# Two of the five wide column groups of each feed-forward input product formed from seven block products

## The chip, the core and the metric

The kernel runs on one core of one Trainium2 chip. Its engines work side by side, each through its own queue of instructions in order: the tensor engine (PE, which also loads weights, PEld), the vector engine (DVE), the scalar engine (ACT), GpSimd (POOL), and the queue that starts DMA transfers (SP). The metric is the device time of one launch in microseconds (us), from which runs of two kernels are compared. Times below are from the span's start unless said otherwise.

## The reference, cut to what matters

Four residual layers over 256 tokens of width 1024. Each has a token mixer with one wide input projection, a memory cross-attention, one output projection, and then a dense SwiGLU feed-forward:

```
def _swiglu(x, w_in, w_out):
    gu = x @ w_in
    return (jax.nn.silu(gu[..., :D_FF]) * gu[..., D_FF:]) @ w_out
...
        x = x + jnp.concatenate([mix, mo], axis=-1) @ w_o[i]
        x = x + _swiglu(_rmsnorm(x, g_ffn[i]), w_ffn_in[i], w_ffn_out[i])
```

`D_FF` is 2816, so `w_ffn_in` of a layer is 1024 x 5632: 2816 gate columns and 2816 up columns. All weights and activations are float32.

## The kernel before, in words

**Precision by parts.** Every large product is made from parts: a weight chunk `raw` is loaded (512 KB), ACT rounds it to `whi` (line 128), DVE forms the rest `wlo = raw - whi` (line 129), and PE adds three matmuls per 128 x 512 block, `hi*hi`, `hi*lo`, `lo*hi` (lines 133 to 135). The activations are transposed and split the same way once for each layer half (`transposed`, line 242: PE transposes, DVE writes `xg`, ACT `xth`, DVE `xtl`).

**Buffers.** `raw` has 3 buffers, `whi` and `wlo` have 8 each; so at most 8 chunks can stand split ahead of PE. PSUM is two pools of 4 banks: `acc` for the large products and `tr` for transposes and attention.

**The input product of the feed-forward.** The 2816 columns are taken in groups b = 0 to 4 of 512 and one of 256 (line 738). For a wide group, `proj` (line 154) runs over the gate columns and then over the up columns. One `proj` loads 4 chunks of 2 x 128 rows, and makes two passes over them, one for each half of the tokens (t = 0, 1): 8 row blocks x 3 matmuls = 24 matmuls a pass, 96 for a group. A chunk's buffer comes free when the second pass has gone over it. After a gate pass ACT forms `sg = silu(gate)` (line 752); after an up pass DVE multiplies (line 754). `hidden` (line 757) is put off by one `flush`: PE transposes the result, ACT and DVE split it into `hh` and `hl` for the output product `out_proj`.

**What sets the order.** The code is written in program order with work put off by `later` and `flush`; a scheduler then places the instructions on each engine's queue, by its own costs and by the buffers that are free. Each engine takes its queue in order, so an instruction that waits holds up all behind it. The waits between engines are set from the data and the buffers.

Of the kernel before, what the change touches and what calls it, by code (L numbers as in the profile page):

```python
# [9 lines left out]
F32 = mybir.dt.float32  # L10
F32R = mybir.dt.float32r
BF16 = mybir.dt.bfloat16
# [5 lines left out]
P = 128  # L18
# [13 lines left out]
NEG = -1e30  # L32

# [6 lines left out]
def trunk_kernel(ctx, tc, x, mem, vecs, w_in, w_kv, w_o, w_f1, w_f2, lams, g_final, out):  # L40
# [3 lines left out]
    wraw = pool("wraw", 3)  # L44
# [5 lines left out]
    ps_acc = pool("ps_acc", 4, space=PSUM)  # L50
    ps_x = pool("ps_x", 4, space=PSUM)
# [4 lines left out]
    warm = work.tile([P, 512], BF16, name="warm", tag="mk")  # L56
    nc.vector.memset(warm, 0.0)

    def warm_up(n):
        ps = ps_x.tile([P, 512], F32, name="warm_ps", tag="tr")  # L60
        for _ in range(n):
            nc.tensor.matmul(ps, warm[:, :P], warm, start=True, stop=True)
# [21 lines left out]
    tmp = work.tile([P, 3, P], F32, name="tmp", tag="att", bufs=6)[:, 0, :]  # L84
# [14 lines left out]
    def alibi(hh0):  # L99

        dist = work.tile([P, 3, P], F32, name="dist", tag="att", bufs=6)
# [14 lines left out]
    def wchunk(srcs, nk, ncol, ahead=False):  # L116
        if ahead:
            raw = big.tile([P, nk, ncol], F32, name="raw", tag="big")
        else:
            raw = wraw.tile([P, nk, ncol], F32, name="raw", tag="raw")  # L120
        c = 0
        for s in srcs:
            n = s.shape[1]
            nc.sync.dma_start(raw[:, :, c:c + n], s.rearrange("(c p) n -> p c n", p=P))
            c += n
        hi = wsplit.tile([P, nk, ncol], F32R, name="whi", tag="whi")
        lo = wsplit.tile([P, nk, ncol], F32R, name="wlo", tag="wlo")
        nc.scalar.copy(hi, raw)  # L128
        wlast[:] = [nc.vector.tensor_tensor(lo, raw, hi.bitcast(F32), ALU.subtract)]  # L129
        return hi, lo  # L130
# [9 lines left out]
    def later(rounds, f):  # L140
        pend.append([rounds, f])
# [12 lines left out]
    def proj(cols, xT, evac, start=None):  # L154

        ncol = sum(s.shape[1] for s in cols)
        nk = 1 if start else 2 if ncol == 512 else 4
        ch = []

        def load(c):  # L160
            ch.append(wchunk([s[c:c + nk * P, :] for s in cols], nk, ncol, start is not None))

        def mms(ps, t, kc):
            hi, lo = ch[kc // nk]
            return mm3(ps[:, :ncol], xT[t][0][:, kc, :], xT[t][1][:, kc, :], hi[:, kc % nk, :],
                       lo[:, kc % nk, :], kc == 0, kc == NKD - 1)

        ps = None
        done = 0
        if start:  # L170
            ps = ps_acc.tile([P, 512], F32, name="acc", tag="acc")
            done = 3
            with tc.issue_after(head[0][1]):
                load(0)
            with tc.issue_after(head[1][0]), tc.issue_after(head[1][1]):
                for kc in range(1, done):
                    load(kc * P)
            for kc in range(done):
                last = mms(ps, 0, kc)
            start(last.ins)  # L180
        for c in range(done * P, D, nk * P):
            load(c)
        for t in range(NT):
            if ps is None:
                ps = ps_acc.tile([P, 512], F32, name="acc", tag="acc")
# [6 lines left out]
            ps, done = None, 0  # L192

    def out_proj(w, order, lhs, lag, evac, settle=None):

        acc = [[ps_acc.tile([P, 512], F32, name="acc", tag="acc") for _ in range(2)] for _ in range(NT)]
        chunks = [2 * kp + k for kp in order for k in range(2)]
        n = len(chunks)

        def mms(t, h, j, ch):  # L200
            lh, ll = lhs(chunks[j], t)
            sl = slice(h * 512, (h + 1) * 512)
            mm3(acc[t][h], lh, ll, ch[0][:, 0, sl], ch[1][:, 0, sl], j == 0, j == n - 1)

        tail = []
        for j, kc in enumerate(chunks):
            ch = wchunk([w[kc * P:(kc + 1) * P, :]], 1, D)
            if j < n - 2 * lag:
                for t in range(NT):
                    for h in range(2):  # L210
                        mms(t, h, j, ch)
                flush()
            else:
                tail.append((j, ch))
        if settle is not None:
            settle()
        for t in range(NT):
            for h in range(2):
                for j, ch in tail:
                    mms(t, h, j, ch)  # L220
                flush()
                evac(t, h, acc[t][h])
# [9 lines left out]
    def stats(src):  # L232
        junk = work.tile([P, D], BF16, name="junk", tag="junk", bufs=1)
# [8 lines left out]
    def transposed(dst, src, gcol, h):  # L242

        th, tl = dst
        ps = ps_x.tile([P, 4, P], F32, name="tr", tag="tr")
# [6 lines left out]
        nc.vector.tensor_tensor(xg, ps, g, ALU.mult)  # L252
        return (nc.scalar.copy(th[:, sl, :], xg).ins,  # L253
                nc.vector.tensor_tensor(tl[:, sl, :], xg, th[:, sl, :].bitcast(F32), ALU.subtract).ins, last_pe)

    def to_T(src, dst, eng):

        ps = ps_x.tile([P, 4, P], F32, name="tr", tag="tr")
# [16 lines left out]
    def mem_kv(i):  # L275
# [3 lines left out]
        def evac(t, ps):  # L279
            kn = work.tile([P, MEMW], F32, name="mk", tag="mk")  # L280
# [4 lines left out]
        def keys(t, kn):  # L285
            tr = ps_x.tile([P, 4, P], F32, name="tr", tag="tr")
# [7 lines left out]
    def mem_attention(qT, kv):  # L294
# [5 lines left out]
        def probs(t):  # L300
            prob = work.tile([P, 4, S], F32, name="mprob", tag="mprob", bufs=1)
# [3 lines left out]
            pss = [ps_x.tile([P, 2, S], F32, name="at", tag="tr") for _ in range(2)]  # L305
# [17 lines left out]
        def turn(t, prob):  # L323
            for j0 in (0, 2):
                tr = ps_x.tile([P, 4, P], F32, name="tr", tag="tr")
# [9 lines left out]
        def values():  # L335
            for pr in range(2):
                ps = ps_x.tile([P, 2, S], F32, name="at", tag="tr")
# [32 lines left out]
    def sb_scores(qT, kT, a, then):  # L370
        zs, us = {}, {}

        def logits(h):
            z = ps_x.tile([P, 4, P], F32, name="at", tag="tr")
            nc.tensor.matmul(z[:, 0:2, :], kT[:, h, 0:P], qT[:, h, :], start=True, stop=True)  # L375
            nc.tensor.matmul(z[:, 2, :], kT[:, h, P:], qT[:, h, P:], start=False, stop=True, skip_group_check=True)
            ab = work.tile([P, 3, P], F32, name="sb_a", tag="att", bufs=6)
# [5 lines left out]
            uh = work.tile([P, 3, P], F32R, name="sb_uh", tag="att", bufs=6)  # L383
            ul = work.tile([P, 3, P], F32R, name="sb_ul", tag="att", bufs=6)
# [4 lines left out]
        def weights(h):  # L389
# [4 lines left out]
            p = work.tile([P, 3, P], F32, name="sb_p", tag="sb_p", bufs=5)  # L394
# [17 lines left out]
    def sb_values(a, v, c0, oh, ol):  # L412
        def heads(hs):
            for h in hs:
                ps = ps_x.tile([P, 4, P], F32, name="at", tag="tr")
# [11 lines left out]
    def diff_scores(qT, kT, hh0, lam, res, then):  # L427
        diffs = []
        abias = alibi(hh0)
        for e in range(2):  # L430
# [4 lines left out]
            for c in range(2):  # L435
                s = ps_x.tile([P, 4, P], F32, name="at", tag="tr")
# [3 lines left out]
                p = work.tile([P, 3, P], F32, name="df_p", tag="att", bufs=6)  # L440
# [17 lines left out]
        def turn():  # L458
            for p1 in diffs:
                tr = ps_x.tile([P, 4, P], F32, name="tr", tag="tr")  # L460
                for b in range(3):
                    nc.tensor.transpose(tr[:, b, :], p1[:, b, :], ident)
                aT = work.tile([P, 3, P], F32, name="sb_p", tag="sb_p", bufs=5)
# [6 lines left out]
    def diff_values(aTs, v, c0, oh, ol, ghead):  # L470
        ons = []
        for e in range(2):
            aT = aTs[e]
            cs = slice(c0 + e * 256, c0 + (e + 1) * 256)
            ps = ps_x.tile([P, NT, 256], F32, name="at", tag="tr")
# [12 lines left out]
        def turn():  # L488
            for e, on in enumerate(ons):
                tr = ps_x.tile([P, 4, P], F32, name="tr", tag="tr")  # L490
# [12 lines left out]
    def conv_mix(cT, uT, oh, ol, half):  # L503
        for c in range(4):
            kc = 4 * half + c
            w = [vec[:, V_CONV + 8 * k + kc:V_CONV + 8 * k + kc + 1] for k in range(3)]
            y = work.tile([P, S], F32, name="cy", tag="mk")
# [8 lines left out]
    def final():  # L516
# [4 lines left out]
        def evac(t, h, acc):  # L521
            sl = slice(h * 512, (h + 1) * 512)
            nc.vector.tensor_tensor(xs[t][:, sl], acc, xs[t][:, sl], ALU.add)
            junk = work.tile([P, D], BF16, name="junk", tag="junk", bufs=1)
# [44 lines left out]
    def load_mem():  # L569
        for t, mt in enumerate(mem_in):  # L570
# [5 lines left out]
            junk = work.tile([P, D], BF16, name="junk", tag="junk", bufs=1)  # L576
# [26 lines left out]
    for i in range(DEPTH):  # L603
# [10 lines left out]
        def memory():  # L614
            mqT = big.tile([P, 2, 2, S], F32R, name="mqT", tag="big")

            def evac(t, ps):
                n = work.tile([P, MEMW], F32, name="mk", tag="mk")
# [3 lines left out]
            def queries(t, n):  # L622
                tr = ps_x.tile([P, 4, P], F32, name="tr", tag="tr")
# [97 lines left out]
        def residual(gcol, nxt, rnx):  # L721
            def evac(t, h, acc):
# [4 lines left out]
                later(1, lambda: transposed(nxt[t], xs[t], gcol, h))  # L727
# [4 lines left out]
        nxt, rnx = [], []  # L732
        out_proj(w_o[i], [4, 0, 1, 2, 3], o_lhs, 2, residual(V_FFN + 8 * i, nxt, rnx), drain)
# [4 lines left out]
        for b in range(6):  # L738
# [18 lines left out]
            def hidden(t, s, hh, hl, n):  # L757
                tr = ps_x.tile([P, 4, P], F32, name="tr", tag="tr")
# [9 lines left out]
            if n == 512:  # L768
                proj([gcols], xT, lambda t, ps: h_out(t, ps, None))
                proj([ucols], xT, lambda t, ps: h_out(t, None, ps))  # L770
            else:
                proj([gcols, ucols], xT, lambda t, ps: h_out(t, ps[:, :n], ps[:, n:2 * n]))

# [39 lines left out]
```

## Time and profile before

| what | value |
|---|---|
| time, median of 3 runs | 1306.28 us (1306.04 to 1307.22) |
| the profiled execution's own time | 1305.36 us |
| its span | 1303.7 us |
| granted PE clock, whole span | 0.999 |
| DVE busy in the span | 762.2 us |
| ACT busy in the span | 672.3 us |
| HBM read | 225.23 MB |

The profile is of one execution. "Busy" of an engine is the sum of its instructions' durations; matmuls overlap one another in the array, so a matmul's duration is longer than the time between two starts. A row of the timeline gives the start, the duration, the engine, the source line, the output and inputs, and in brackets how long the engine stood idle before it and whom it waited for.

### The profile page before, as it was taken

Reading aid. Unit: us, or ns where it says so; the run is one execution under the profiler, and the core shown is the slowest. Engines: PE = TensorE matmul, PEld = TensorE weight load, DVE = VectorE, ACT = ScalarE, POOL = GpSimd, SP = SyncE. Lnnn points to the kernel's source line nnn. Section 1 sums busy time; section 2 is a strip of 40 time slices with the busy share of each in tenths; the row PEclk is TensorE's granted clock in tenths of the full one; section 3 lists DMA queues with packets and bytes.
Section 4 is the critical chain, followed back from the end, with each engine's and each line's share of the span. In section 5 each row is a group of like instructions: output and inputs, shape, how many; then the busy total and the mean of one; then the engine's idle time right before and its main releaser. Section 6 shows DMA issues by size and latency. Waiting matters only on the chain.

```text
span 1303.7 us, 16267 instructions
## 1 busy us (share of the span) xinstructions
PE 1288.5 (99%) x6175; PEld 1065.3 (82%) x6175; DVE 762.2 (58%) x955; ACT 672.3 (52%) x943; POOL 52.0 (4%) x109
## 2 busy tenths in 40 slices
PE   8899999999999999999999999999999999999997
PEld 6788888888888888888888888888888888888886
DVE  5675565655576656555457776555546655655542
ACT  6656454444456545444445455444436755544441
POOL 1000000000101000000000000000000001000001
PEclk9999999999999999999999999999999999999999
DMA  6654565657564456665655565656665445656571
GB/s 243 194 155 136 162 193 178 188 177 218 152 186 123 144 162 194 194 193 179 202 154 174 174 185 172 187 176 186 209 190 171 129 129 162 187 183 184 183 220 44
DMA packets 107790, 227.34 MB, mean 174 GB/s; under 512 B 7488, under 2 KB 20288, under 8 KB 107712
## 3 DMA queue, kind: packets, MB, share of 16 engines
q1 hardware_dynamic: 107712, 226.31, 56.8%
q8 instruction: 48, 0.79, 0.2%
q14 instruction: 30, 0.25, 0.1%
HBM read 225.23 MB, written 1.05 MB: 174 GB/s over the span
## 4 chain that ended last, share of the span: by engine, by line
PE 93%; DMA 3%; DVE 2%; ACT 1%; issue 0%; POOL 0%; SPq 0%; POOLq 0%; ACTq 0%; DVEq 0%
PE acc L133 28%; PE acc L135 28%; PE acc L134 28%; DMA raw<-in_w_in 2%; PE tr L760 1%; PE tr L248 1%; PE tr L260 1%; DVE wlo L129 1%; PE at L341 1%; ACT whi L128 1%; PE tr L328 1%; PE at L309 1%; PE at L417 1%; PE at L392 0%; PE at L375 0%
## 5 line engine op out<-in xcount | busy, mean ns | idle before, releaser
L129 DVE TENSOR_TENSOR wlo<-raw,whi 128x1024 fp32r<-128x1024 f32 (+1 forms) x428 | 518.5, 1215 | 395.5 <-ACT whi L128 386.7
L128 ACT CAST whi<-raw 128x1024 fp32r<-128x1024 f32 (+1 forms) x428 | 445.0, 1044 | 415.4 <-PE acc L135 265.2
L133 PE MATMUL acc<-whi,xth 128*128 128x512 f32 (+1 forms) x1152 | 454.0, 394 | 1.2 <-ACT xth L253 1.2
L134 PE MATMUL acc<-wlo,xth 128*128 128x512 f32 (+1 forms) x1152 | 442.5, 384 | 1.8 <-DVE wlo L129 1.8
L135 PE MATMUL acc<-whi,xtl 128*128 128x512 f32 (+1 forms) x1152 | 443.4, 385 | 0.0
L135 PEld LDWEIGHTS acc<-whi,xtl 128*128 128x128 f32 x1152 | 216.4, 188 | 44.0
L134 PEld LDWEIGHTS acc<-wlo,xth 128*128 128x128 f32 x1152 | 217.0, 188 | 42.6 <-DVE wlo L129 3.0
L133 PEld LDWEIGHTS acc<-whi,xth 128*128 128x128 f32 x1152 | 216.7, 188 | 42.2 <-ACT xth L253 1.7
L133 PE MATMUL acc<-whi,hh 128*128 128x512 f32 x320 | 125.4, 392 | 0.0
L135 PE MATMUL acc<-whi,hl 128*128 128x512 f32 x320 | 124.6, 389 | 0.0
L134 PE MATMUL acc<-wlo,hh 128*128 128x512 f32 x320 | 124.6, 389 | 0.0
L135 PEld LDWEIGHTS acc<-whi,hl 128*128 128x128 f32 x320 | 60.1, 188 | 12.6
L133 PEld LDWEIGHTS acc<-whi,hh 128*128 128x128 f32 x320 | 60.1, 188 | 12.2
L134 PEld LDWEIGHTS acc<-wlo,hh 128*128 128x128 f32 x320 | 60.1, 188 | 12.1
L752 ACT ACTIVATE sg<-acc,rstd 128x512 f32<-128x512 f32 (+1 forms) x48 | 31.4, 654 | 49.5 <-PE acc L135 49.5
L133 PE MATMUL acc<-whi,oh 128*128 128x512 f32 x128 | 51.1, 399 | 0.0
L135 PE MATMUL acc<-whi,ol 128*128 128x512 f32 x128 | 50.0, 391 | 0.0
L134 PE MATMUL acc<-wlo,oh 128*128 128x512 f32 x128 | 49.9, 390 | 0.0
L754 DVE SCALAR_TENSOR_TENSOR sg<-acc,rstd,sg 128x512 f32<-128x512 f32 (+1 forms) x48 | 33.8, 703 | 26.6 <-PE acc L135 18.8
L235 ACT ACTIVATE junk<-x 128x1024 bf16<-128x1024 f32 x16 | 16.9, 1058 | 36.8 <-DVE x L724 36.5
L228 POOL TENSOR_SCALAR rstd<-ss 128x1 f32<-128x1 f32 x16 | 5.3, 334 | 640.2 <-ACT junk L235 640.1
L724 DVE TENSOR_TENSOR x<-acc,x 128x512 f32<-128x512 f32 x28 | 19.3, 688 | 18.9 <-PE acc L135 18.4
(185 smaller groups left out, 1071.0 us busy)
## 6 DMA issues: line engine op xcount, KB each, us to landing
raw<-in_w_ffn_in SPq DMA_DIRECT2D x160, 512.0 KB, 4.3
raw<-in_w_in SPq DMA_DIRECT2D x100, 512.0 KB, 4.2
raw<-in_w_ffn_out SPq DMA_DIRECT2D x88, 512.0 KB, 4.3
raw<-in_w_o SPq DMA_DIRECT2D x40, 512.0 KB, 4.4
raw<-in_w_mem_kv SPq DMA_DIRECT2D x16, 512.0 KB, 3.8
raw<-in_w_ffn_in SPq DMA_DIRECT2D x32, 256.0 KB, 3.7
raw<-in_w_in SPq DMA_DIRECT2D x8, 256.0 KB, 6.2
x<-in_x SPq DMA_DIRECT2D x4, 256.0 KB, 4.0
```

The lines of the kernel that those rows point to most:

```text
L128: nc.scalar.copy(hi, raw)
L129: wlast[:] = [nc.vector.tensor_tensor(lo, raw, hi.bitcast(F32), ALU.subtract)]
L133: nc.tensor.matmul(ps, lh, wh, start=first, stop=False)
L134: nc.tensor.matmul(ps, lh, wl, start=False, stop=False)
L135: return nc.tensor.matmul(ps, ll, wh, start=False, stop=last)
L235: nc.scalar.activation(junk, src, AF.Square, accum_out=ss)
L248: last_pe = nc.tensor.transpose(ps[:, c, :], src[:, kc * P:(kc + 1) * P], ident).ins
L260: nc.tensor.transpose(ps[:, c, :], src[:, c * P:(c + 1) * P], ident)
L309: nc.tensor.matmul(pss[r][:, pr, :], qT[r * 64:(r + 1) * 64, a, pr, t * P:(t + 1) * P], kT[r * 64:(r + 1) * 64, b, pr, :], start=a + b == ...
L724: nc.vector.tensor_tensor(xs[t][:, sl], acc, xs[t][:, sl], ALU.add)
L752: nc.scalar.activation(s, g_ps, AF.Silu, scale=rx[t])
L754: nc.vector.scalar_tensor_tensor(s, u_ps, rx[t], s, ALU.mult, ALU.mult)
```

## The change

For b = 1 and b = 4 of every layer the two `proj` calls are replaced by `winograd`, Strassen's scheme in a form with shared sums. It treats [gate columns | up columns] of the group as a 2 x 2 block matrix: the rows of the weights in two halves of 512 (`b11`, `b21` gate, `b12`, `b22` up), against the tokens in two halves and their 1024 channels in two halves. Seven products of blocks take the place of eight. A product is 4 row blocks x 3 matmuls = 12 matmuls, in two steps (s = 0, 1) of 6; a group has 84.

Three kinds of work come with it. Four sums of weight blocks are formed on DVE in each step (`plus`, 128 x 1024), before their split. `tokens_side` makes four sums of token blocks once for each layer, and splits them. `h_sums` puts the seven accumulators together into gate and up on DVE. The seven accumulators of a group live in seven PSUM banks, so the two PSUM pools become one of 8 banks. `raw` gets 7 buffers instead of 3, and most small work tiles share one set of 12 (`att`). The bytes that are loaded stay the same.

```
-    wraw = pool("wraw", 3)
+    wraw = pool("wraw", 7)
...
-    ps_acc = pool("ps_acc", 4, space=PSUM)
-    ps_x = pool("ps_x", 4, space=PSUM)
+    ps_x = ps_acc = pool("ps", 8, space=PSUM)
...
+    def winograd(left, right, ab, evac):
+        acc = {}
+        def product(p, w, s):
+            if s == 0:
+                acc[p] = ps_acc.tile([P, 512], F32, name="acc", tag="ps")
+            lh, ll = ab[p]
+            for k in range(2):
+                kc = 2 * s + k
+                mm3(acc[p], lh[:, kc, :], ll[:, kc, :], w[0][:, k, :], w[1][:, k, :], kc == 0, kc == 3)
+            if s == 1:
+                evac(p, acc)
...
+        def plus(out, a, b):
+            nc.vector.tensor_tensor(out, a, b, ALU.add)
+        for s in range(2):
+            b11, b12 = (load(c, 2 * s * P) for c in (left, right))
+            b21, b22 = (load(c, 512 + 2 * s * P) for c in (left, right))
+            product(1, wparts(b11), s)
+            t = wraw.tile([P, 2, 512], F32, name="wsum", tag="raw")
+            plus(t, b11, b12)
+            product(5, wparts(t), s)
+            flush()
+            product(2, wparts(b21), s)
+            plus(t, t, b22)
+            product(6, wparts(t), s)
+            flush()
+            plus(b12, b12, b22)
+            product(7, wparts(b12), s)
+            product(3, wparts(b22), s)
+            flush()
+            plus(t, t, b21)
+            product(4, wparts(t), s)
...
+            if b in (1, 4):
+                def h_sums(p, acc, sums=sums, sg=sg, hh=hh, hl=hl):
+                    def up(t, c):
+                        nc.vector.scalar_tensor_tensor(sg[t], c, rneg[t], sg[t], ALU.mult, ALU.mult)
+                        later(2, lambda: hidden(t, sg[t], hh, hl, 512))
+                    if p == 1:
+                        nc.scalar.copy(sums["v"], acc[1])
+                    elif p == 2:
+                        tt(sg[0], acc[2], sums["v"], ALU.add)
+                        nc.scalar.activation(sg[0], sg[0], AF.Silu, scale=rx[0])
+                    elif p == 6:
+                        tt(sums["u"], acc[6], sums["v"], ALU.add)
+                        tt(sums["x"], acc[5], sums["u"], ALU.add)
+                    elif p == 7:
+                        tt(sums["u"], acc[7], sums["u"], ALU.add)
+                        tt(sums["y"], acc[5], sums["u"], ALU.add)
+                    elif p == 3:
+                        tt(sums["x"], acc[3], sums["x"], ALU.add)
+                        up(0, sums["x"])
+                    elif p == 4:
+                        tt(sg[1], acc[4], sums["u"], ALU.add)
+                        nc.scalar.activation(sg[1], sg[1], AF.Silu, scale=rx[1])
+                        up(1, sums["y"])
+                winograd(gcols, ucols, ab, h_sums)
```

On DVE, where group b = 1 of the first layer ended and b = 2 began, this stood before. `wlo_2028` is the last up chunk of b = 1, `wlo_2097` to `wlo_2115` are the four gate chunks of b = 2, and `sg_1922` is the first multiply of b = 1.

```order
L129 TENSOR_TENSOR wlo_2028<-raw_2025,whi_2027 128x1024
L764 TENSOR_TENSOR hl_1751<-tr_1961,hh_1750 128x4x128
L129 TENSOR_TENSOR wlo_2097<-raw_2094,whi_2096 128x1024
L129 TENSOR_TENSOR wlo_2103<-raw_2100,whi_2102 128x1024
L129 TENSOR_TENSOR wlo_2109<-raw_2106,whi_2108 128x1024
L129 TENSOR_TENSOR wlo_2115<-raw_2112,whi_2114 128x1024
L754 SCALAR_TENSOR_TENSOR sg_1922<-acc_2031,rstd_1523,sg_1922 128x512
```

At the same place of the DVE queue now: `wlo_1933`, `wlo_1946` and `wlo_1959` are the splits of products 7, 3 and 4 in step 1 of b = 1, and `wlo_1978` is the first gate chunk of b = 2.

```order
L859 TENSOR_TENSOR sg_1773<-acc_1818,sv_1890 128x512
L132 TENSOR_TENSOR wlo_1933<-raw_1874,whi_1932 128x1024
L863 TENSOR_TENSOR su_1927<-acc_1830,sv_1890 128x512
L132 TENSOR_TENSOR wlo_1946<-raw_1878,whi_1945 128x1024
L864 TENSOR_TENSOR sx_1928<-acc_1800,su_1927 128x512
L132 TENSOR_TENSOR wlo_1959<-wsum_1892,whi_1958 128x1024
L867 TENSOR_TENSOR su_1927<-acc_1842,su_1927 128x512
L870 TENSOR_TENSOR sx_1928<-acc_1853,sx_1928 128x512
L868 TENSOR_TENSOR sy_1942<-acc_1800,su_1927 128x512
L852 SCALAR_TENSOR_TENSOR sg_1773<-sx_1928,rneg_1767,sg_1773 128x512
L873 TENSOR_TENSOR sg_1774<-acc_1865,su_1927 128x512
L132 TENSOR_TENSOR wlo_1978<-raw_1975,whi_1977 128x1024
```

The next group's first split stood ahead of all of the group's multiplies; now it stands behind the whole putting together of the group (`L859` to `L873`), of which the last, `L873`, waits for the last product.

At the end of b = 4, DVE goes on to the narrow group b = 5, whose four chunks are `wlo_2525`, `wlo_2532`, `wlo_2539` and `wlo_2546`.

```order
L864 TENSOR_TENSOR sx_2475<-acc_2347,su_2474 128x512
L132 TENSOR_TENSOR wlo_2532<-raw_2528,whi_2531 128x1024
L867 TENSOR_TENSOR su_2474<-acc_2389,su_2474 128x512
L870 TENSOR_TENSOR sx_2475<-acc_2400,sx_2475 128x512
L868 TENSOR_TENSOR sy_2489<-acc_2347,su_2474 128x512
L852 SCALAR_TENSOR_TENSOR sg_2320<-sx_2475,rneg_1767,sg_2320 128x512
L873 TENSOR_TENSOR sg_2321<-acc_2412,su_2474 128x512
L132 TENSOR_TENSOR wlo_2539<-raw_2535,whi_2538 128x1024
L852 SCALAR_TENSOR_TENSOR sg_2321<-sy_2489,rneg_1769,sg_2321 128x512
L132 TENSOR_TENSOR wlo_2546<-raw_2542,whi_2545 128x1024
```

Here two of the next group's four chunks stand ahead of the last sums and two behind them; before, all four stood ahead of the first multiply of b = 4.

On SP, the queue that starts the loads, this stood early in the program before: `raw_313` is the last chunk of the first key projection, `memn` the memory tokens, `raw_437` the first chunk of the values, `raw_547` that of the memory keys and values.

```order
L124 DMA raw_313<-in_w_in 128x2x512
L566 DMA memn_291<-in_mem 128x1024
L566 DMA memn_293<-in_mem 128x1024
L124 DMA raw_437<-in_w_in 128x2x512
L124 DMA raw_443<-in_w_in 128x2x512
L124 DMA raw_449<-in_w_in 128x2x512
L124 DMA raw_455<-in_w_in 128x2x512
L124 DMA raw_547<-in_w_mem_kv 128x2x512
```

The same place now, where `raw_310` is the last key chunk and `raw_434` the first of the values:

```order
L124 DMA raw_310<-in_w_in 128x2x512
L124 DMA raw_434<-in_w_in 128x2x512
L124 DMA raw_440<-in_w_in 128x2x512
L124 DMA raw_446<-in_w_in 128x2x512
L124 DMA raw_452<-in_w_in 128x2x512
L640 DMA memn_288<-in_mem 128x1024
L640 DMA memn_290<-in_mem 128x1024
L124 DMA raw_544<-in_w_mem_kv 128x2x512
```

The loads of the values moved ahead of the memory tokens.

More of the change, by code (lines that the diff above doesn't have):

```diff
@@ new lines, in tokens_side, with parts @@
+    def tokens_side(xg, xT):
+        a11, a12, a21, a22 = xg[0][0], xg[0][1], xg[1][0], xg[1][1]
+        half = lambda t, h: tuple(x[:, 4 * h:4 * h + 4, :] for x in xT[t])
+        ab = {1: half(0, 0), 2: half(0, 1), 4: half(1, 1)}
+        tt, stt = nc.vector.tensor_tensor, nc.vector.scalar_tensor_tensor
+        def parts(src):
+            hi = work.tile([P, 4, P], F32R, name="sh", tag="att", bufs=NATT)
+            lo = work.tile([P, 4, P], F32R, name="sl", tag="att", bufs=NATT)
+            nc.scalar.copy(hi, src)
+            tt(lo, src, hi.bitcast(F32), ALU.subtract)
+            return hi, lo
+        tt(a22, a22, a21, ALU.subtract)
+        ab[5] = parts(a22)
+        tt(a21, a11, a21, ALU.subtract)
+        ab[7] = parts(a21)
+        stt(a11, a22, -1.0, a11, ALU.mult, ALU.subtract)
+        ab[6] = parts(a11)
+        stt(a12, a12, -1.0, a11, ALU.mult, ALU.subtract)
+        ab[3] = parts(a12)
+        return ab
@@ L194, in out_proj @@
     def out_proj(w, order, lhs, lag, evac, settle=None):
-        acc = [[ps_acc.tile([P, 512], F32, name="acc", tag="acc") for _ in range(2)] for _ in range(NT)]
+        acc = [[ps_acc.tile([P, 512], F32, name="acc", tag="ps") for _ in range(2)] for _ in range(NT)]
         chunks = [2 * kp + k for kp in order for k in range(2)]
@@ L726, in evac @@
                     nxt.append(xt_tiles())
[L727 removed]
+                    if keep is not None:
+                        keep.append([])
+                later(1, lambda: transposed(nxt[t], xs[t], gcol, h, None if keep is None else keep[t]))
                 if h == 1:
@@ L772, in trunk_kernel @@
                 proj([gcols, ucols], xT, lambda t, ps: h_out(t, ps[:, :n], ps[:, n:2 * n]))
+            if b == 0:
+                ab = tokens_side(xg, xT)
+                rneg = []
+                for t in range(NT):
+                    r = small.tile([P, 1], F32, name="rneg", tag="rneg")
+                    nc.vector.tensor_scalar(r, rx[t], -1.0, None, ALU.mult)
+                    rneg.append(r)
         def f_lhs(kc, t):
```

93 lines of the change are left out of this document (54 added, 39 removed).

## The prediction

> **What bounds the kernel now.** I read the page's busy line and its chain first, then the timeline of PE in the feed-forward of the first layer, since that is where the change sits.
>
> ```profile
> PE 1288.5 (99%) x6175; PEld 1065.3 (82%) x6175; DVE 762.2 (58%) x955; ACT 672.3 (52%) x943; POOL 52.0 (4%) x109
> PE 93%; DMA 3%; DVE 2%; ACT 1%; issue 0%; POOL 0%; SPq 0%; POOLq 0%; ACTq 0%; DVEq 0%
> L133 PE MATMUL acc<-whi,xth 128*128 128x512 f32 x1088 | 435.6, 401 | 1.2 <-ACT xth L253 1.2
> 171.52 0.39 PE L133 MATMUL acc<-whi,xth 128*128 128x512 f32 x1
> 176.74 0.39 PE L135 MATMUL acc<-whi,xtl 128*128 128x512 f32 x1
> 185.13 0.60 PE L760 MATMUL tr<-ident,sg 128*128 128x128 f32 x4
> 185.48 0.48 PE L133 MATMUL acc<-whi,xth 128*128 128x512 f32 x1
> 188.34 0.39 PE L133 MATMUL acc<-whi,xth 128*128 128x512 f32 x1
> ```
>
> PE is the chain, and it hardly ever waits. But what a matmul costs is not its duration of 0.39 to 0.40 us. The rows at 171.52 and 176.74 are the first and the last of the 24 matmuls of one pass, so one starts every 5.22 / 23 = **0.227 us**. By the duration, 96 matmuls would be worth 38 us; by the distance of starts, 21.8. Four transposes cost 0.35 (185.13 to 185.48). Group b = 1 of the first layer starts at 188.34.
>
> Next the two engines that feed PE, and the same stage by windows (columns: length, then busy time and count of PE, PEld, DVE, ACT, POOL, the clock, the DMA share, GB/s).
>
> ```profile
> L129 DVE TENSOR_TENSOR wlo<-raw,whi 128x1024 fp32r<-128x1024 f32 x420 | 513.1, 1225 | 394.6 <-ACT whi L128 385.9 <-PE tr L625 0.6
> L128 ACT CAST whi<-raw 128x1024 fp32r<-128x1024 f32 x420 | 440.1, 1052 | 409.3 <-PE acc L135 265.2 <-DMA raw<-in_w_ffn_in 59.3 <-DMA raw<-in_w_in 23.3
> L754 DVE SCALAR_TENSOR_TENSOR sg<-acc,rstd,sg 128x512 f32<-128x512 f32 x40 | 29.9, 748 | 18.8 <-PE acc L135 18.8
> L724 DVE TENSOR_TENSOR x<-acc,x 128x512 f32<-128x512 f32 x28 | 19.3, 688 | 18.9 <-PE acc L135 18.4
> L254 DVE TENSOR_TENSOR xtl<-xg,xth 128x512 fp32r<-128x512 f32 x32 | 22.2, 697 | 6.8 <-ACT xth L253 6.6
> 188.30:211.10 22.80, 22.80 (x106) 18.84 (x105) 12.55 (x13) 10.97 (x13) 0.00 (x0) 1.00 0.61 187
> 45.54 2.36 DVE L129 TENSOR_TENSOR wlo<-raw,whi 128x1024 fp32r<-128x1024 f32 x2
> 47.81 0.56 DVE L381 SCALAR_TENSOR_TENSOR sb_a<-at,sb_a 128x384 f32<-128x384 f32 x1
> 166.14 0.69 DVE L252 TENSOR_TENSOR xg<-tr,vec 128x512 f32<-128x512 f32 x1
> 166.74 0.68 DVE L724 TENSOR_TENSOR x<-acc,x 128x512 f32<-128x512 f32 x1
> 171.71 1.22 DVE L129 TENSOR_TENSOR wlo<-raw,whi 128x1024 fp32r<-128x1024 f32 x1
> ```
>
> In a group of 22.8 us DVE works 12.55 and ACT 10.97: a chunk is split in 1.1 us and serves PE for 12 matmuls, 2.7 us. Rows of a full DVE queue follow faster than they last: two splits fill 45.54 to 47.81, **1.14 us each**, and a row of 512 fills 166.14 to 166.74, **0.60**. A three-operand row (0.748) I take at 0.66, by the same overlap.
>
> **The change: what goes.** 12 matmuls for each group, two groups, four layers: 96 x 0.227 = **21.8 us** of PE. The DMA bytes stay.
>
> **What comes, and on whom.** In a Strassen group PE needs 84 x 0.227 + 0.35 = 19.4 us. DVE needs 14 splits and 8 sums of weight blocks at 1.14 (25.1), 7 sums of accumulators at 0.60 and two multiplies at 0.66 (5.5), two `hl` (1.2): about 32 us. A split chunk now serves PE for 6 matmuls, 1.36 us, and costs DVE 1.14 plus 4/7 of a sum, 1.8. So for these 19 us **DVE is the slower engine**, and the 8 split buffers decide how far it gets ahead. ACT has 14 casts and five smaller rows, about 18 us, and just keeps pace.
>
> *First group (b = 1).* DVE comes to its first new row (`L256`) when the last split of b = 0 is through, 171.71 + 1.14 = 172.85. Up to and with the first split of b = 2, which the order puts behind `L873`, there stand 15 splits and 8 sums (26.2 us), 15 rows of 512 with `tokens_side` among them (9.0), 5 three-operand rows (3.3) and one small (0.1): 38.6. One wait inside can't be avoided: the split of product 6 in step 1 comes right behind the sum it splits, and ACT's cast (1.052 less overlap) lies between, 1.0 us. So that split ends at 172.85 + 38.6 + 1.0 = 212.5. PE without a wait would ask for it at 188.34 + 19.4 + 0.23 = 208.0. PE is 4.6 us late, with the restart. 0.35 of that is filled by transposes that stood elsewhere before, and b = 2's third chunk comes 0.1 late behind the second multiply: **4.3 us given back** against 2.7 won. After that b = 2 and b = 3 leave DVE some 10 us each, so nothing is carried on.
>
> *Second group (b = 4).* No `tokens_side`, and DVE starts from a full set of buffers. Its last wait is for the buffer of b = 3's first up chunk, free after six matmuls of the last pass; with the cast that is 3.15 us before b = 4 begins. Then 9 splits, 4 sums, two rows of 512 and a multiply stand up to the first row of `h_sums` (`L859`): 16.7 us, so DVE is there 13.55 us after the group's start. Product 2 is complete at 14.25 (10 products, a transpose, 0.26 until the result is seen), so DVE waits 0.7 us. From there the rows up to the third chunk of b = 5 (`wlo_2539`) are 4 splits, 7 sums, 1 multiply, 9.4 us after product 2's result, which is 0.26 after its last matmul's successor starts. PE comes there after 4 products, 2 chunks, a transpose and one matmul, 8.75. Late by 1.05 with the restart; the fourth chunk is late by 0.7, its multiply waiting on ACT's silu. **1.8 us given back.**
>
> The four layers' orders on DVE and ACT are alike row by row in this stage, so both count four times: 17.2 and 7.2 us.
>
> *The front.* More `raw` buffers and the loads of the values moved ahead touch the waits between 40 and 60 us.
>
> ```profile
> 41.96 0.38 PE L375 MATMUL at<-qT,kT 128*128 128x256 f32 x1
> 43.95 0.49 PE L376 MATMUL at<-qT,kT 128*128 128x128 f32 x2 [1.40 <-DVE kT L264]
> 56.92 0.39 PE L135 MATMUL acc<-whi,meml 128*128 128x512 f32 x1
> 59.57 0.44 PE L392 MATMUL at<-sb_uh,ntri 128*128 128x384 f32 x1 [2.26 <-ACT sb_uh L385]
> 49.64 1.05 ACT L128 CAST whi<-raw 128x1024 fp32r<-128x1024 f32 x1 [1.98 <-DMA raw<-in_w_in]
> 52.48 1.05 ACT L128 CAST whi<-raw 128x1024 fp32r<-128x1024 f32 x1 [1.38 <-DMA raw<-in_w_in]
> 55.00:60.00 5.00, 2.74 (x12) 1.82 (x11) 3.28 (x4) 3.56 (x7) 1.69 (x2) 1.00 0.66 197
> ```
>
> PE loses 1.99 - 0.23 and 2.65 - 0.23, 4.2 us in all. ACT's queue waited 1.98 + 1.38 us for loads ahead of the `sb_uh` that the second gap waits for; with 7 buffers those loads start earlier, and that gap should go. In the first, one split (1.14) no longer stands ahead of the `kT` copy. **3.4 us won**, between 0 and 4.2.
>
> *Not shown by any row:* the sum of two weight blocks, all SBUF, float32 out. Its nearest row is the split, the same operation and size (1.14); lower end 0.60, as if at twice the rate; upper end 1.35, a three-operand row of that size and a wait on the row before. I take 1.14. At 0.60 the 8 sums of b = 1 shrink by 4.3 us and the stall is gone (-17 us in four layers); at 1.35 b = 1 ends 1.7 us later (+7). In b = 4 no sum of weights stands between `L859` and the late splits, so either end moves only its margin of 0.7.
>
> The Trainium skill, page "VectorE: DVE Perf Modes", section "The perf-mode tier table", has a two-tensor operation on fp32 at one element a cycle even in SBUF, and only one-source operations at two. By it the sum stays as it is and the lower end falls away; by the rows alone 0.60 stays possible, since none shows this operation.
>
> PSUM in one pool costs nothing that I can find: when product 4's accumulator opens, seven others were taken, and the transposes' bank was emptied 3 us before.
>
> **Sum.** 1305.36 (the profiled execution) - 21.8 + 17.2 + 7.2 - 3.4 = 1304.6. The median of the runs is 0.9 above that execution: **1305.5 us**, no change that can be told. About 0.2% (2.6 us) is what a measurement of this kernel tells from none.
>
> **Rivals.**
>
> *DVE keeps up.* If the lag at the group ends is a half of what I worked out (sums nearer to 0.9 us, or fewer exposed casts), 12 us come back: 1293. For it: DVE is only 58% busy over the span. Against it: 32 us of rows in 19.4 us of PE, and 8 buffers. Fully hidden it would be 1281, and by the matmuls' durations, 38 us instead of 21.8, even 1265; the sum of DVE's rows speaks against the one, the distance of starts against the other.
>
> *The casts are exposed more often (slower).* Eight products of a group split a sum that DVE has just made, so ACT's cast (1.05) lies between two DVE rows each time; I counted one exposed hop in b = 1 and none in b = 4. The point from which it decides is b = 4's margin of 0.7 us and ACT's load of 18 in 19.4: once ACT is behind, every hop shows. Three more in each group cost 3 x 1.05 x 8 = 25, less 3 for margins: 1328. For it: L129 waited 385.9 us for `whi` in the span, its main wait. Against it: other rows stand between most pairs.
>
> *The clock falls in the gaps (slower).* The row of 55 to 60 us shows PE idle for 2.65 us and the clock at 1.00. The longest single gap I expect is about 1.5 us, so nothing. Were it half for some 3.4 us behind each of the 8 group ends, it would cost 8 x 1.7 = 14 us, 1319. The Trainium skill, page "TensorE: Matmul & The Clock Gate", section "Why this matters for your kernels", warns of the half rate after idle gaps over about 3 us; no gap here is that long before the change.
>
> *The front gains nothing:* 1308.9. It is inside the forecast's own range, 1300 to 1311.
>
> **Chances.** Forecast 0.45; DVE keeps up, at least by half, 0.25; casts exposed 0.25; clock 0.05. For eight in ten the range reaches into both neighbours, 1288 to 1324. Faster by over 0.2% (under 1303.7): all of the second case and about a quarter of the forecast's, 0.37. Within: 0.27. Slower: both last cases and the forecast's top, 0.36.
>
> **What would show it.** Right: PE gaps of 4 to 5 us in sum just behind each b = 1 and of about 2 behind each b = 4, waiting on `wlo`; DVE near 100% from 173 to 213; a pitch of 1.14 for the sums; no gap at 57. Wrong: gaps inside the groups rather than behind them (casts), or hardly any (DVE ahead); a clock under 1.00.

## The result, and the profile after

The changed kernel takes **1335.03 us** (median of 4, 1333.75 to 1336.26) against 1306.16 of the kernel before in the same comparison: ratio 1.0222, 95% interval 1.0204 to 1.0239. It is slower by 29 us; the forecast was 1305.5, and the range ended at 1324. The profiled execution has a span of 1334.5 us, 30.8 more than before.

The page of the changed kernel: the busy line, the clock by slices, and the chain.

```profile
PE 1290.3 (97%) x6079; PEld 1056.6 (79%) x6079; DVE 930.3 (70%) x1163; ACT 721.1 (54%) x1015; POOL 60.0 (4%) x109
PEclk9989999999999999999998999999999899999999
PE 76%; DVE 16%; issue 3%; ACT 2%; DMA 1%; SPq 0%; POOL 0%; POOLq 0%; ACTq 0%; DVEq 0%
```

PE has fewer matmuls, yet the chain is only 76% PE, and the clock row has an 8 in three slices. The waits of PE in the whole span (total, times, longest) say on whom it waited:

```profile
PE acc L136 <- ACT whi L131: 17.6, 4, 4.4
PE acc L137 <- DVE wlo L132: 13.4, 21, 1.1
PE tr L836 <- DVE sg L852: 4.1, 4, 1.0
```

The second and third rows are, for the most part, the group ends that the prediction spoke of. The first is four waits of 4.4 us that it did not. One lies in each layer's mixer; PE's timeline in the first:

```profile
85.18 1.03 PE L402 MATMUL tr<-ident,mprob 128*128 128x128 f32 x8
86.14 0.97 PE L383 MATMUL at<-mkT,mqT 64*128 64x256 f32 x12
91.52 0.80 PE L136 MATMUL acc<-whi,xth 128*128 128x512 f32 x1 [4.41 <-ACT whi L131]
92.11 0.63 PE L334 MATMUL tr<-ident,qkn 128*128 128x128 f32 x2
93.11 0.80 PE L137 MATMUL acc<-wlo,xth 128*128 128x512 f32 x1 [0.36 <-DVE wlo L132]
```

Behind the wait a matmul lasts 0.63 to 0.80 us instead of 0.39. The windows (length, then busy time and count of each engine, clock, DMA share, GB/s) have for 90 to 105 us in the changed kernel

```profile
90.00:105.00 15.00, 13.12 (x52) 10.04 (x54) 11.27 (x16) 10.11 (x15) 0.00 (x0) 0.77 0.61 194
```

and in the kernel before

```profile
90.00:105.00 15.00, 15.00 (x93) 11.77 (x92) 11.40 (x22) 8.26 (x20) 0.00 (x0) 1.00 0.50 148
```

So a stall costs its 4.8 us of waiting and then some 3 us more at half clock. The stages are told apart by starts of the same PE work in both timelines:

| stage | rows compared | after minus before, layers 1 to 4 (us) | sum |
|---|---|---|---|
| front | first scores of the memory attention, 78.18 for 82.65 | -4.5 | -4.5 |
| mixers | from there (L309, now L383) to the values (L341, now L415); first layer 82.65 to 101.31, now 78.18 to 104.60 | +7.8, +7.6, +8.0, +8.0 | **+31.4** |
| b = 1 | first `sg` transposes of b = 0 to those of b = 2; first layer 185.13 to 230.58, now 188.75 to 237.28 | +3.1, +1.5, +1.6, +2.9 | +9.2 |
| b = 4 | from the first `sg` transposes of b = 2 to the last `sg` transposes of b = 5; first layer to 293.57, now 299.46 | -0.8, -1.5, -1.7, -0.8 | -4.8 |

Together 31.3, of 30.8 in the span. The mixers are the loss: the other three stages cancel one another.

**Why the mixers.** The diff holds a line that the account of the change leaves out and that the prediction gave no term: `mprob`, the probabilities of the memory attention, left its own buffer and takes its turn among `raw`'s seven.

```
-            prob = work.tile([P, 4, S], F32, name="mprob", tag="mprob", bufs=1)
+            prob = wraw.tile([P, 4, S], F32, name="mprob", tag="raw")
```

ACT's queue in the first mixer shows what follows. Before, the casts stand between the exponentials (`L316`) of the two token halves; `whi_955` to `whi_973`, of the chunks used first, stand further ahead:

```
L128 CAST whi_1073<-raw_1071 128x1024
L316 ACTIVATE mprob_844,msm_846<-at_847,mmx_845 128x256 x2
L316 ACTIVATE mprob_844,msm_846<-at_848,mmx_845 128x256 x2
L128 CAST whi_1079<-raw_1077 128x1024
L128 CAST whi_1085<-raw_1083 128x1024
...
L316 ACTIVATE mprob_921,msm_923<-at_924,mmx_922 128x256 x2
```

Now six casts, from that of the very next projection (`whi_952`) on, stand behind both, and so it is in all four mixers:

```
L390 ACTIVATE mprob_918,msm_920<-at_921,mmx_919 128x256 x2
L390 ACTIVATE mprob_918,msm_920<-at_922,mmx_919 128x256 x2
L131 CAST whi_952<-raw_950 128x1024
L131 CAST whi_958<-raw_956 128x1024
...
L131 CAST whi_1076<-raw_1074 128x1024
```

The timeline of DVE, ACT and SP beside PE's wait:

```profile
87.14 1.29 DVE L386 TENSOR_REDUCE mmx<-at 128x2 f32<-128x512 f32 x2
88.60 0.47 ACT L390 ACTIVATE mprob<-at,mmx 128x256 f32<-128x256 f32 x1 [1.98 <-DVE mmx L387]
90.41 5.78 ACT L131 CAST whi<-raw 128x1024 fp32r<-128x1024 f32 x6
51.96 10.53 SPq L124 DMA_DIRECT2D raw<-in_w_in  x3
86.24 8.34 SPq L124 DMA_DIRECT2D raw<-in_w_in  x3
```

PE computes the scores (86.14), DVE their maximum (87.14), ACT the exponentials (88.60), and only then ACT casts the chunk for PE's next matmul (90.41). Five of the six chunks' loads had been started by 62.5 us, so it isn't data that is missing: a chain of three engines that used to run beside the projection now stands ahead of it in ACT's order. The sixth load did wait, until the transposes `L402` had freed the first `mprob`. That the casts stand there because buffers of one set are handed out in program order, and `mprob` asks before the next chunks, is my reading of the order; that they stand there only while `mprob` is in the set, the experiments show.

### The profile page after: what moved, and what is told of

It reads as the page before. It is cut to its first block, busy times and chain, and to the rows that moved or that the text cites. A ratio compares the mean times of both kernels' runs of the same rounds, so it can differ in the third digit from the quotient of the medians.

```text
span 1334.5 us, 16363 instructions
## 1 busy us (share of the span) xinstructions
PE 1290.3 (97%) x6079; PEld 1056.6 (79%) x6079; DVE 930.3 (70%) x1163; ACT 721.1 (54%) x1015; POOL 60.0 (4%) x109
## 4 chain that ended last, share of the span: by engine, by line
PE 76%; DVE 16%; issue 3%; ACT 2%; DMA 1%; SPq 0%; POOL 0%; POOLq 0%; ACTq 0%; DVEq 0%
PE acc L137 23%; PE acc L138 23%; PE acc L136 23%; DVE wlo L132 7%; DVE wsum L221 2%; ACT whi L131 1%; PE tr L334 1%; DMA raw<-in_w_ffn_out 1%; PE tr L836 1%; PE tr L320 1%; DVE raw L221 1%; DVE sl L253 1%; PE at L415 1%; PE at L449 1%; PE at L491 1%
## 5 line engine op out<-in xcount | busy, mean ns | idle before, releaser
L131 ACT CAST whi<-raw 128x1024 fp32r<-128x1024 f32 (+1 forms) x428 | 436.9, 1042 | 277.0 <-PE acc L138 215.5
L136 PE MATMUL acc<-whi,xth 128*128 128x512 f32 (+1 forms) x992 | 396.5, 400 | 18.0 <-ACT whi L131 17.6
L137 PE MATMUL acc<-wlo,xth 128*128 128x512 f32 (+1 forms) x992 | 388.0, 391 | 13.4 <-DVE wlo L132 13.4
L138 PE MATMUL acc<-whi,xtl 128*128 128x512 f32 (+1 forms) x992 | 385.5, 389 | 0.0
L136 PEld LDWEIGHTS acc<-whi,xth 128*128 128x128 f32 x992 | 189.6, 191 | 56.1 <-ACT whi L131 20.1
L137 PEld LDWEIGHTS acc<-wlo,xth 128*128 128x128 f32 x992 | 189.8, 191 | 54.1 <-DVE wlo L132 20.1
L136 PE MATMUL acc<-whi,hh 128*128 128x512 f32 x320 | 125.4, 392 | 0.0
L131 ACT CAST whi<-wsum 128x1024 fp32r<-128x1024 f32 x48 | 50.5, 1052 | 55.8 <-DVE wsum L221 52.0
L136 PEld LDWEIGHTS acc<-whi,hh 128*128 128x128 f32 x320 | 60.1, 188 | 12.2
L132 DVE TENSOR_TENSOR wlo<-wsum,whi 128x1024 fp32r<-128x1024 f32 x48 | 58.5, 1218 | 5.9 <-ACT whi L131 5.5
L137 PE MATMUL acc<-wlo,sh 128*128 128x512 f32 x128 | 50.7, 396 | 0.7
L136 PE MATMUL acc<-whi,oh 128*128 128x512 f32 x128 | 51.1, 399 | 0.0
L138 PE MATMUL acc<-whi,sl 128*128 128x512 f32 x128 | 49.9, 390 | 0.0
L136 PE MATMUL acc<-whi,sh 128*128 128x512 f32 x128 | 49.2, 389 | 0.0
```

The source lines that it names most:

```text
L136: nc.tensor.matmul(ps, lh, wh, start=first, stop=False)
L137: nc.tensor.matmul(ps, lh, wl, start=False, stop=False)
L138: return nc.tensor.matmul(ps, ll, wh, start=False, stop=last)
```

## The experiments

Theory A: `mprob` among `raw`'s buffers costs the 31 us. B: the single PSUM pool and the shared small tiles do. C: Strassen itself does. Times are medians; each ratio is to the kernel before on the same chip.

**1. `mprob` in its own buffer** (6 `raw` buffers, to make room).

```
-    wraw = pool("wraw", 7)
+    wraw = pool("wraw", 6)
-            prob = wraw.tile([P, 4, S], F32, name="mprob", tag="raw")
+            prob = work.tile([P, 4, S], F32, name="mprob", tag="mprob", bufs=1)
```

> The changed kernel with one edit: mprob gets a work buffer of its own again, and raw 6 buffers instead of 7 to make room. Theory A (the ring): mprob sits among raw's buffers, so the load that is given mprob's buffer waits until the transposes L402 have read it, and every later load waits behind it on SP; the four waits of about 4.4 us on whi in the mixers, with the half clock behind them, are worth 31.4 us. Expected 1335.0 - 31.4 = 1303.6 us, give or take 2 for the buffer less; no PE wait on whi over 1 us and a clock of 1.00 from 75 to 105 us. Theory B (one PSUM pool and one set of small tiles): the mixers lose because scores, transposes and accumulators take turns in 8 banks. Expected 1335 +- 2, the waits stay. Theory C (Strassen itself): 1335, since nothing of it is changed.

Measured: 1307.76 us, ratio 1.0011 (1.0002 to 1.0020). PE's waits:

```profile
PE acc L137 <- DVE wlo L132: 12.0, 19, 1.1
PE tr L836 <- DVE sg L852: 4.1, 4, 1.0
PE acc L136 <- ACT xth L327: 1.5, 1, 1.5
```

The first mixer's window:

```profile
90.00:105.00 15.00, 15.00 (x82) 11.58 (x81) 9.35 (x18) 8.69 (x18) 0.00 (x0) 1.00 0.43 134
```

The four waits and the half clock are gone with one tile out of the set; as causes of the 31 us, B and C fall. The expectation took the held-up load for the cause. By the rows above, the chunk that PE waits for had been loaded, and it is the place of its cast on ACT that costs. The time is 4 us above what A gave: by the starts of the table, the feed-forward stages cost 6.5 us here against 4.4, and the mixers 1.4.

**2. Only that line, in the kernel before** (`raw` 4 instead of 3, `mprob` among them).

> The kernel before (no Strassen, two PSUM pools of 4, its own tags) with one edit: mprob takes its turn among raw's buffers, which are 4 instead of 3, so the bytes stay the same. Theory A: the mixers stall as in the changed kernel, four times by at least 4 us and the half clock behind: 1306.2 + 31 = 1337 us, at least 1326. Theories B and C: 1306 +- 2, since neither the PSUM pool nor Strassen is there.

Measured: 1324.33, ratio 1.0142 (1.0127 to 1.0158). Without any Strassen, PE stalls again in each mixer, here at the transposes of `mprob`:

```profile
PE tr L328 <- DVE mprob L320: 10.7, 3, 3.6
PE tr L328 <- ACT whi L128: 3.8, 1, 3.8
```

A holds in kind, but 18 us is under its 20. By the first scores of the memory attention (78.02 for 82.65), the front gains 4.6 us here too, which the expectation left out; so the rest of the kernel loses some 23. The waits are 0.6 to 0.8 us shorter, and the clock, at half for 6.8 us behind each wait in the changed kernel, is at half for as long in the first layer only (0.50 from 89.30 to 96.10) and for half as long in the other three (0.75 over 6.8 us).

**3 and 4. No Strassen**, with `mprob` in the set, and out of it.

```
-            if b in (1, 4):
+            if b in ():
```

> The changed kernel with all five wide groups by proj: no Strassen and no sums of tokens, but its buffers, tags and PSUM pool. From the lag of the one trace behind the other, b = 1 cost 9.2 us in the four layers and b = 4 gained 4.8, so theories A and B expect 1335.0 - 4.4 = 1330.6 us with the four long waits on whi in place. Theory C expects the time to fall back to 1302 to 1306.

> Both edits: mprob in a buffer of its own with 6 for raw, and no Strassen. Theory A expects the kernel before less what the front won in the changed trace (4.5 us): 1301.5 us, so Strassen as it stands would be worth about +2 us beside own6. Theory B expects 1330, the waits in the mixers staying. Theory C expects 1302 to 1306.

Measured: 1330.41, ratio 1.0189 (1.0175 to 1.0202), and 1301.81, ratio 0.9968 (0.9956 to 0.9981). Both are within 0.3 us of A; B had the first as well, but not the second. `PE acc L136 <- ACT whi L131` is 17.6 us in the first and absent in the second. So the buffers other than `mprob`'s win 4.5 us (the front), and Strassen as it stands loses 4 to 6, more than the 2 that was expected.

**5 and 6. Strassen in one group**, `b in (4,)` or `b in (1,)`, with `mprob` apart.

> mprob in its own buffer, raw 6, Strassen in b = 4 alone. Theory A with the lags of the trace: b = 4 gained 0.8 to 1.7 us a layer, 4.8 in all, so 1301.8 - 4.8 = 1297.0 us. If the gain of b = 4 were only what b = 1 had pushed on to it, it would be 1301.8 or more.

> The same with Strassen in b = 1 alone. b = 1 cost 1.5 us in two layers and 3 in the two where the clock fell behind it, 9.2 in all: 1301.8 + 9.2 = 1311.0 us; with no fall of the clock 1308; if b = 1 and b = 4 share one cost (DVE's backlog carried on), 1302.

Measured: 1298.55, ratio 0.9951 (0.9939 to 0.9964), and 1311.32, ratio 1.0048 (1.0035 to 1.0062). The times are within 1.6 us of what was worked out, but for b = 4 this flatters it: the kernel before is 1.5 us faster on this chip (1304.86 for 1306.33), and by the ratios b = 4 gains about 2 us over run 4 (0.9951 for 0.9968, whose intervals overlap). By the starts of the stages it gains 0.8 to 0.9 us in each layer, 3.2 in all, and not 4.8. With b = 1 alone, the stage of b = 4 takes 63.0 us in every layer, as before: b = 1 hands no cost on, and the two groups don't share one. b = 4 alone is faster than the kernel before and than the changed one.

**7. Strassen in b = 2 and 4**, so that `tokens_side` lies under an ordinary group.

> The same with Strassen in b = 2 and b = 4: the sums of tokens and their splits, 8 DVE rows and more, now stand under b = 1, an ordinary group that leaves DVE some 10 us. If the 4.3 us behind b = 1 came from tokens_side on top of the group's own rows, b = 2 behaves as b = 4 and the time is 1301.8 - 9.6 = 1292 us. If they come from the group's own rows and the place of the next group's splits behind the last sums, b = 2 costs as b = 1 did: 1301.8 + 9.2 - 4.8 = 1306.

Measured: 1301.12, ratio 0.9968 (0.9956 to 0.9981): between the two, and the same as run 4 without any Strassen. Of the first layer's waits:

```profile
230.94 0.50 PE L137 MATMUL acc<-wlo,xth 128*128 128x512 f32 x1 [0.88 <-DVE wlo L132]
232.86 0.66 PE L836 MATMUL tr<-ident,sg 128*128 128x128 f32 x4 [0.26 <-DVE sg L852]
273.84 0.66 PE L836 MATMUL tr<-ident,sg 128*128 128x128 f32 x4 [0.50 <-DVE sg L852]
275.58 0.50 PE L137 MATMUL acc<-wlo,xth 128*128 128x512 f32 x1 [1.08 <-DVE wlo L132]
```

Without `tokens_side` beside it a group's end waits less than b = 1's did (1.6 us in sum for 2.4), but behind b = 4 PE waits longer than with b = 4 alone (1.9 us for 1.3). That one ordinary group between does not let DVE catch up wholly is a likely reason, not tested by itself.

**8. The wait filled** with 18 matmuls that nobody reads, `mprob` in the set.

```
             prob = probs(1)
+            fps = ps_x.tile([P, 4, P], F32, name="fill", tag="ps")
+            for _ in range(18):
+                nc.tensor.matmul(fps, fillx[0][0][:, 0, :], fillx[0][0][:, 0:4, :], start=True, stop=True)
```

> The changed kernel, mprob still in raw's ring, with 18 matmuls of 512 columns that nobody reads put into PE's queue right where it waits for whi in each mixer. At 0.227 us between starts they fill 4.1 us of the wait of 4.41. If the half clock behind the wait comes from PE standing idle, it stays at 1.00 and some 3 us a mixer come back (14 matmuls at 0.43 instead of 0.227): 1335.0 - 12 = 1323 us. If the clock falls from something else there (the burst of loads), 1335 and the clock of 90 to 105 us still at 0.77. If the fill is worked off before the wait begins or after it, the time rises by 4 x 4.1 = 16.

Measured: 1327.57, ratio 1.0169 (1.0155 to 1.0182), 4.6 us above what was expected. On PE's timeline the fill in the second layer, and a wait that is new there:

```profile
386.32 4.37 PE L429 MATMUL fill<-xth 128*128 128x512 f32 x18
...
411.54 0.30 PE L539 MATMUL tr<-ident,df_p 128*128 128x128 f32 x1 [2.71 <-DVE df_p L531]
```

The first mixer's window:

```profile
90.00:105.00 15.00, 14.82 (x80) 11.21 (x79) 13.11 (x20) 11.29 (x18) 0.00 (x0) 1.00 0.70 241
```

The clock stays at 1.00, and second scores to values shrink by 3.0 us in the first mixer (86.09 to 101.58, for 86.14 to 104.60): the fall came from PE standing idle, and is worth what was said. In the second layer some 4.5 us are given back at the new wait and a half clock behind it: the run was 4.9 us ahead of the changed kernel at that layer's first scores, won 2.7 in the stall, and was 3.1 ahead at its feed-forward. Why that wait came is open.

**9 and 10. One of four sums of weights on POOL**, with b = 1 and 4, and with b = 4 alone.

```
-            plus(b12, b12, b22)
+            nc.gpsimd.tensor_tensor(b12, b12, b22, ALU.add)
```

> mprob in its own buffer, raw 6, Strassen in b = 1 and 4, and in each step one of the four sums of weight blocks (b12 + b22, for product 7) on POOL instead of DVE: 2 x 1.14 us of DVE a group less. If DVE's sum of rows sets both group ends, the 2.4 us of waits behind b = 1 and the 1.2 to 1.4 behind b = 4 nearly go: 1307.8 - 4 x 3.3 - 2 for a clock that no longer falls = 1293 us. POOL's sum is estimated at 2.6 us, twice the 1.29 us of its row of 128x512 at L602; product 7 comes some 5 us after its loads, so it should be covered. If POOL's sum takes much longer than that or slows DVE while it runs, product 7 waits, and the time is 1308 or more.

> The same with Strassen in b = 4 alone. The waits of 1.3 us behind b = 4 go, the matmuls saved (2.7 us) stay: 1298.6 - 4 x 1.2 = 1293.8 us. If the last two splits of b = 5 are late by their place behind the last sum (L873) and not by the rows ahead of it, 1298.6.

Measured: 1323.10, ratio 1.0138 (1.0120 to 1.0156), and 1308.75, ratio 1.0025 (1.0016 to 1.0034): slower by 15 and 10 us than with DVE. Run 9's groups of POOL's sums and of DVE's splits `sl`:

```profile
L235 POOL TENSOR_TENSOR raw<-raw 128x1024 f32<-128x1024 f32 x16 | 48.1, 3008 | 328.3 <-DVE wsum L221 256.7 <-DVE sg L830 53.6 <-DMA raw<-in_w_ffn_in 18.0
L253 DVE TENSOR_TENSOR sl<-xg,sh 128x512 fp32r<-128x512 f32 x16 | 19.5, 1220 | 0.0
```

The same `sl` in run 1:

```profile
L253 DVE TENSOR_TENSOR sl<-xg,sh 128x512 fp32r<-128x512 f32 x16 | 10.9, 684 | 0.0
```

And run 9's timeline where the first of these sums runs:

```profile
170.54 3.99 POOL L235 TENSOR_TENSOR raw<-raw 128x1024 f32<-128x1024 f32 x1 [3.21 <-DVE wsum L221]
...
172.24 2.85 DVE L253 TENSOR_TENSOR sl<-xg,sh 128x512 fp32r<-128x512 f32 x1
```

POOL's sum takes 3.0 us in the mean, and a DVE row beside it 2.85 instead of 0.68. What DVE is spared it loses again: it has 16 rows fewer and is busy for 936.0 us, for 931.8 in run 1. How the 15 us come about from there was not followed; by the starts, some 10 of them are lost in the stage of b = 4.

**11 and 12. The next group's first chunks split ahead of the last evacuation**: two of them with b = 1 and 4, and three with b = 4 alone.

```
             plus(t, t, b21)
-            product(4, wparts(t), s)
+            parts = wparts(t)
+            if s == 1:
+                ahead = [wchunk(*n) for n in nxt]
+            product(4, parts, s)
```

> mprob in its own buffer, raw 6, Strassen in b = 1 and 4 with all sums on DVE, and the first two chunks of the next group loaded and split ahead of product 4's evacuation, so that on DVE behind b = 1 both splits stand ahead of L873 instead of behind it. If the place behind L873 makes the split late, some 1 us a layer comes back behind b = 1: 1303.8 us. If DVE's sum of rows sets it, one row of 0.6 us and the wait on the last product change places: within 1306 to 1308.5.

> mprob in its own buffer, raw 6, Strassen in b = 4 alone, and three of the four chunks of b = 5 loaded and split ahead of product 4's evacuation: on DVE the third split stands ahead of L873 and the fourth ahead of the second multiply. From the rows of the run without this, the third split ends 0.6 us earlier (one row of 512) and the fourth 1.3 (that row and the wait of 0.6 for silu), so the waits of 0.88 and 0.38 behind b = 4 shrink by about 1 us a layer: 1298.6 - 4 = 1294.6 us. Against it: the second multiply ends 0.45 us later, and its transposes had 0.2 us of margin; if they become what PE waits for, the gain is lost and the time stays at 1298 to 1299.

Measured: 1303.54, ratio 0.9989 (0.9980 to 0.9998), and 1299.83, ratio 0.9951 (0.9937 to 0.9965). The first gains 3 to 4 us on run 1 (by the ratios, by the medians). Behind b = 1 the wait on the first split falls from 1.08 to 0.48 us:

```profile
208.17 0.50 PE L138 MATMUL acc<-wlo,xth 128*128 128x512 f32 x1 [0.48 <-DVE wlo L133]
```

The time is the 1303.8 that was expected for the place behind `L873`, but not by 1 us in every layer. By the starts, b = 1 is 1.9 and 2.1 us shorter in the first two layers, where the clock had fallen in run 1's trace and no longer does; in the other two it is 0.4 us longer and 0.8 shorter. So most of the gain stands where the clock stays up, and the number came out in part by luck. The second gains nothing; its first layer:

```profile
277.00 0.50 PE L138 MATMUL acc<-wlo,xth 128*128 128x512 f32 x1 [0.29 <-DVE wlo L133]
281.29 0.66 PE L842 MATMUL tr<-ident,sg 128*128 128x128 f32 x4 [1.15 <-DVE sg L858]
```

The wait on the split falls from 0.88 (run 5) to 0.29, and the transposes wait 1.15 us on the multiply that moved back: one wait replaced by another, as its expectation allowed.

## Why the prediction was wrong, by its own steps

**The step that failed** is the one on buffers, "The front": "More `raw` buffers and the loads of the values moved ahead touch the waits between 40 and 60 us." Beyond that the prediction gave the buffers no price, and said of PSUM that it "costs nothing that I can find". It read the new order of DVE at the group ends and of SP in the front, but not ACT's and DVE's in the mixers, where `mprob` had entered `raw`'s set. That one line, put at nothing, is +31.4 us of the table; taken out, 27 to 29 of them come back (runs 1 and 4 against the changed kernel and run 3).

**Matmuls saved, 21.8; b = 1, 17.2 given back; b = 4, 7.2 given back.** Right in mechanism, and nearly in size where the clock stayed up. Net, b = 1 was to lose 1.6 us a layer and lost 1.5 and 1.6 in the two middle layers; b = 4 was to gain 0.9 and gained 0.8 to 1.7. DVE in b = 1 of the first layer:

```profile
176.16 0.68 DVE L256 TENSOR_TENSOR xg<-xg 128x512 f32<-128x512 f32 x1
188.57 1.21 DVE L221 TENSOR_TENSOR raw<-raw 128x1024 f32<-128x1024 f32 x1
189.70 1.21 DVE L221 TENSOR_TENSOR wsum<-wsum,raw 128x1024 f32<-128x1024 f32 x1
204.31 1.22 DVE L132 TENSOR_TENSOR wlo<-wsum,whi 128x1024 fp32r<-128x1024 f32 x1 [1.20 <-ACT whi L131]
214.97 2.34 DVE L132 TENSOR_TENSOR wlo<-raw,whi 128x1024 fp32r<-128x1024 f32 x2
```

From `L256` to the end of the first split of b = 2 it is 39.95 us (214.97 + 1.14 - 176.16), against 39.65 worked out, with the one exposed cast (1.20) where it was put. The sum of two weight blocks cost what was taken: two of them start 1.13 us apart (188.57 and 189.70).

**The front, 3.4 won:** 4.5, with both gaps gone.

**"The clock falls in the gaps"** had a chance of 0.05 and is a part of the loss, at two places. (The gap that it read as 2.65 us of idle PE was 2.26 by the row at 59.57; 2.65 is the distance of the two starts.) In the mixers it is some 3 us of each 8. Behind b = 1 it costs 1.5 us in the first and last layer. PE's waits there, in the first layer:

```profile
212.04 0.50 PE L137 MATMUL acc<-wlo,xth 128*128 128x512 f32 x1 [0.31 <-DVE wlo L132]
...
214.50 0.66 PE L836 MATMUL tr<-ident,sg 128*128 128x128 f32 x4 [1.03 <-DVE sg L852]
...
216.23 0.50 PE L137 MATMUL acc<-wlo,xth 128*128 128x512 f32 x1 [1.08 <-DVE wlo L132]
```

The windows behind them in the first layer and in the second, where the waits were the same:

```profile
217.00:220.50 3.50, 3.50 (x10) 2.73 (x10) 3.39 (x5) 1.91 (x3) 0.00 (x0) 0.54 0.91 276
...
550.00:554.00 4.00, 4.00 (x20) 3.21 (x20) 4.00 (x5) 1.82 (x2) 0.00 (x0) 1.00 0.87 282
```

The prediction all but excluded it because no single gap would be long; here three short ones of 2.4 us in all were followed by half clock in layers 1 and 4 (0.54 in the first) and not in 2 and 3 (1.00).

**"DVE keeps up" and "casts exposed more often"** did not happen: the waits stood behind the groups, and in b = 1 of the first layer one cast was exposed.

With the mixer's term the same sum gives 1305.5 + 31.4 = 1336.9; 1335.0 was measured. That it comes so near is in part luck: b = 1 cost 2.9 us more than its term, mostly by the clock, and b = 4 and the front won 1.1 more each.

## What to carry to other kernels

A tile moved into another set of buffers can change the order, and not only the space: here it moved six casts behind the exponentials on ACT. Compare the queues of all engines in every stage that the moved tile touches, also where nothing is computed otherwise. And a block product saved on PE pays only as far as the sums it needs fit in the vector engine's spare time of that very stage: one group behind ordinary ones gained a little (0.9951, for 0.9968 with none), two gained nothing or lost (0.9968 and 1.0011).

## What the runs showed of the hardware

- After a PE wait of 4.41 us the clock was at half for about 6 us in all four mixers; a fill of 18 matmuls kept it at 1.00. Waits of 0.31, 1.03 and 1.08 us within 4.5 us were followed by half clock in 7 of 16 cases (the changed kernel and runs 1, 6 and 8), 0.30, 1.03 and 0.48 in none of 4 (run 11). A single wait of 2.71 us was followed by it in run 8 (0.50 from 412.80 to 416.10), one of 2.26 us at 59.57 in the kernel before was not. The Trainium skill, page "TensorE: Matmul & The Clock Gate", section "What's actually happening", has the rate fall after an idle window of about 3.4 us that runs freely. The long waits agree. The short ones, 2.4 us in sum, stayed below that and were still followed by it; here the measurement decides.
- A DVE row that reads two float32 operands in SBUF is held up beside POOL's sum: 2.85 us for a row of 0.68 (run 9). The sum itself took from 2.39 to 3.99 us. The Trainium skill, page "GPSIMD Engine Reference", section "8. Key points", says that the two share their SBUF interfaces; this case agrees.
